# A two-layer trunk on one core: fp32 residual in DRAM, boundary sums on VectorE, a bias table of 32 rows

## The chip, the cores and the metric

The kernel runs on one core of one Trainium2 chip. The metric is the device time of one execution in microseconds (us). The core's engines are TensorE (PE, with its weight loads shown apart as PEld), VectorE (DVE), ScalarE (ACT), GpSimd (POOL) and SyncE (SP); SP, ACT and POOL issue the DMAs.

## The reference

A residual stream h of 512 tokens and 1024 features goes through two layers. The first is a gated linear recurrence (HGRN2), the second differential attention with a relative-position bias; each is followed by a squared-ReLU MLP. Every sub-layer has a norm before and after it. All is float32.

```python
def rms_norm(x, w):
    return x * lax.rsqrt(jnp.mean(x * x, axis=-1, keepdims=True) + EPS) * w

def squared_relu_mlp(h, w_up, w_down):
    u = jax.nn.relu(h @ w_up)
    return (u * u) @ w_down

for layer in range(2):
    if layer == 0:
        mix = hgrn2_mixer(rms_norm(h, a_norm_pre), a_w_in, lb, a_gate_norm, a_w_out)
        h = h + rms_norm(mix, a_norm_post)
    else:
        mix = diff_attn_mixer(rms_norm(h, b_norm_pre), k_sh, v_sh, b_w_q, b_lambda, b_subln, b_w_out, rel_bias, lam_init)
        h = h + rms_norm(mix, b_norm_post)
    ff = squared_relu_mlp(rms_norm(h, mlp_norm_pre[layer]), mlp_w_up[layer], mlp_w_down[layer])
    h = h + rms_norm(ff, mlp_norm_post[layer])
    if layer == 0:
        k_sh, v_sh = shared_kv(h, kv_norm, w_kv)

# in diff_attention, for a block of 128 queries
bias = rel_bias[rel_bucket(k_pos[None, :] - q_pos[:, None])]
logits = q @ k.T * scale + bias          # two maps per head, each with its own softmax
attn = p[:, :, 0] - lam * p[:, :, 1]
```

## The kernel before

Features lie on the partitions and tokens along a row. Every float32 operand of a product is held as two float32r parts, hi and lo, and a product is three matmuls (`mm3`). The residual stream itself is held only as such parts: `xhi[0..3]` and `xlo[0..3]`, each 128 partitions by 2 x 512, so that tile `pr` holds features 256 pr to 256 pr + 255. Weights come from DRAM in pieces of 512 KB on SP's queue into four `raw` buffers (`fetch_w`); ScalarE makes the hi part (`whi`, L172) and VectorE the lo part (`wlo`, L173), into eight buffers each.

The products follow one another in four stages: the mixer of layer 0 with its output products `ao`, the MLP of layer 0 (`up`, then `dn` into `zacc`), the attention with its output products `bo`, the MLP of layer 1. Where a stage ends there is a boundary, done by `bounds`, once for each half of the tokens (h = 0 and 1, 256 tokens each). There are four: ao, m0 (after the first MLP), bo and m1 (after the second MLP, which writes the result; `want` is "out"). Instructions of both m0 and m1 show the name m. A boundary's half goes like this:

- The residual is put together again: `hs = xhi + xlo`, four tiles of 128 x 512, on GpSimd (L268).
- `sums` takes the finished products, squares them on ScalarE and adds the squares (`ssp`): tiles 1 and 2 on GpSimd, tile 3 on VectorE (L290), then the two rows of a tile (L291).
- TensorE turns the squares into a mean on all partitions (`ps_mr`), ScalarE and VectorE make the reciprocal root `ry` (L240 to L252).
- `new` scales the products (L326, two instructions a tile), adds the residual (L327), and splits the sum into xhi (ACT, L331) and xlo (DVE, L332). Of m1's half each, tiles 0 and 1 are added on GpSimd, and the sums go out by DMA (L329).
- `sums` once more, over the new residual (`ssn`), for the next stage's norm: `ps_mr` again, and at m0 also `rb` (ACT, L350) and `ps_rc`.

TensorE's order is written out by `Plan`. It keeps a clock of its own; a chain that waits for other engines yields how long its next product should stay back (the constants W_...), and main work is put in its place. In this order the products of the second token half stand beside the first half's boundary. The other engines' order is made by the scheduler, which prefers instructions of chains (`CHAIN_AHEAD`).

At the start `first_loads` brings x, splits it, and squares it: tiles 0 and 1 on GpSimd (L512), 2 and 3 on ScalarE (L515). The bias of the attention is a row of 640 values for each of 16 maps (`bw`). `params` writes it 128 times over to a DRAM table `bias_dr` of 16 x 128 x 640 by one DMA from GpSimd's queue (L573), while the first MLP runs. `attend` reads it back for each head with a row step of 639, by which each partition gets its row shifted by one more (L834, SP's queue).

Of the kernel before, what the change touches and what calls it, by code (L numbers as in the profile page):

```python
# [17 lines left out]
P = 128  # L18
# [6 lines left out]
NB = 640  # L25
CHAIN_AHEAD = 300

# how long (us) the order of the tensor engine's work leaves a chain to the other engines
W_XSUM, W_XRSTD = 10.0, 6.3                             # x: squares; rstd
W_POST, W_POST_LAST = 4.0, 3.4                          # a post-norm's squares, by half  # L30
W_NEW, W_NEWSUM, W_RSTD = 5.8, 9.7, 4.5                 # new residual: split; squares; rstd
W_GATE_FIRST, W_GATE, W_LEVEL = 10.0, 5.7, 2.15         # recurrence: gates; one level
W_KEYS, W_STATE = 1.5, 0.8                              # recurrence: keys by token; states
W_HEAD, W_STORE = 11.7, 5.5                             # a head's norm; its split
W_QK, W_NEXT, W_P, W_PER_TILE, W_PT = 3.6, 0.94, 5.0, 0.66, 2.5  # attention: q and k; softmax; transposed

# columns of the packed per-feature vectors
# [6 lines left out]
class Plan:  # L44
    """The order of the tensor engine's work: one main stream, and chains that come back to it after a while.

    A generator yields either a number (its next products wait that long, in us, for other engines) or
    a function (it goes on once that is true)."""
# [39 lines left out]
def trunk_kernel(ctx: ExitStack, tc: tile.TileContext, x_t, w_qf, w_g, w_i, w_ao, w_k, w_q, w_v, w_bo, w_up, w_dn,  # L88
# [35 lines left out]
    ulo = [cp.tile([P, 2, S], F32R, name=f"ulo{i}") for i in range(4)]  # L124
    gn = cp.tile([P, G_N], F32, name="gn")
# [20 lines left out]
    bias_dr = dr.tile([16, P, NB], F32, name="bias_dr")  # L146

# [1 line left out]
    def fetch_w(src, ncols, pr, name, pieces=1):  # L149
        """The DMA of 1024 columns' worth of a [128, 8, ncols] block of weights."""  # L150
        per = 1024 // ncols
        raw = wp.tile([P, per, ncols], F32, tag="raw", name=f"raw_{name}_{pr}", bufs=4)
        n = per // pieces
        for i in range(pieces):
            nc.sync.dma_start(raw[:, i * n:(i + 1) * n, :], src[:, per * pr + i * n:per * pr + (i + 1) * n, :])
        return raw

    def split_w(raw, gain, pr, name):
        """Weights (times their gain) in two float32r parts, by rows of 128."""
# [28 lines left out]
    def wmm(ps, wt, kt, c0, xh, xl, lo, hi, start, stop, sk=False):  # L188
        """Weights stationary: ps[feature, token] += w[kt][:, c0:c0+128].T x[kt]."""
        wh, wl = wt[kt]  # L190
        j = kt % 2
        mm3(ps, wh[:, c0:c0 + P], wl[:, c0:c0 + P], xh[kt // 2][:, j, lo:hi], xl[kt // 2][:, j, lo:hi], start, stop, sk)

    def xmm(ps, wt, kt, ncols, t0, start, stop):
        """Tokens stationary: ps[token, feature] += x[kt][:, t0:t0+128].T w[kt]."""
# [4 lines left out]
    def rsqrt_col(ms, add, out, scale=1.0):  # L200
        """out = (ms * scale + add) ** -0.5 on a few columns: a first guess from the exponent, then Newton's steps."""
# [13 lines left out]
    def mean_cols(parts, n, ones):  # L215
        """Sums over the partitions (times ones), tokens on partitions: [128, n / 128] in PSUM."""
# [11 lines left out]
    def mean_rows(parts, n):  # L228
        """Sums over the partitions / D, on every partition: [128, n] in PSUM."""
# [5 lines left out]
    def rsqrt_rows(pool, ms, add):  # L235
        """-2 (ms + add) ** -0.5 on a [128, n] block (add, a block, becomes the sum): a guess from ScalarE's tables, then Newton's step."""
# [18 lines left out]
    def bounds(pool, ps_list, zacc, h, gpost, eab, want, name):  # L255
        """Post-norm of the finished products, residual sum, statistics and split for the next products."""
# [8 lines left out]
        hs = []  # L265
        for pr in range(4):
            r = tl("hs", f"hs{pr}", 4)
            g.tensor_tensor(r, xhs[pr].bitcast(F32), xls[pr].bitcast(F32), op=ALU.add)  # L268
            hs.append(r)

        def sums(src, nm, last=None):
            """Sums of squares over the tiles that src yields (with last: the last tile by halves)."""
            acc = tl("ssum", f"ss{nm}", 2)
            for pr in range(4):
# [14 lines left out]
                if pr > 0:  # L289
                    (v if pr == 3 else g).tensor_tensor(acc, acc, sq, op=ALU.add)  # L290
# [28 lines left out]
        def new(pr, _):  # L319
# [7 lines left out]
            (g if want == "out" and pr < 2 else v).tensor_tensor(t, t, hs[pr], op=ALU.add)  # L327
            if want == "out":
                nc.sync.dma_start(out_t.rearrange("(k p) t -> p k t", p=P)[:, 2 * pr:2 * pr + 2, lo:hi], t)  # L329
                return  # L330
            a.activation(xhs[pr], t, AF.Copy)  # L331
            v.tensor_tensor(xls[pr], t, xhs[pr].bitcast(F32), op=ALU.subtract)  # L332
            return t
# [11 lines left out]
        if want == "ea":  # L345
            # the MLP's products lack the pre-norm's factor: its post-norm takes eps (ms + eps) ** 2 for eps
# [11 lines left out]
    def by_halves(wt, xh, xl, name, before_last=()):  # L358
        """1024 -> 1024 features, weights stationary, tokens by halves: yields between products, keeps the banks."""
        for h, (lo, hi) in enumerate(halves):  # L360
            banks = [mmt(f"{name}_h{h}_{i}") for i in range(4)]
            views = [b.rearrange("p (j t) -> p j t", j=2) for b in banks]
            if h == 1:
                # the last tile in a bank of its own, so that the one before can be read
# [21 lines left out]
    def block(pool, proj, gpost, name, layer, want):  # L386
        """The mixer's output products (proj, from their second half on), its post-norm, and the MLP."""
# [69 lines left out]
    def head_norm(pool, po, add, name):  # L457
        """po [128 tokens, 4, 128 features] in PSUM, normed by token and transposed: [128 features, tokens] in PSUM."""
# [22 lines left out]
    def first_loads(hp):  # L481
        """x and the first head's weights: DMAs, splits and squares, in the order that the products want."""
# [21 lines left out]
        for pr in range(4):  # L504
# [5 lines left out]
            if pr < 2:  # L510
                sq.append(hp.tile([P, 2, S], F32, tag="vt", name=f"sqx{pr}", bufs=2))
                g.tensor_tensor(sq[pr], raws[pr], raws[pr], op=ALU.mult)  # L512
            else:
                sq.append(raws[pr])
                a.activation(sq[pr], raws[pr], AF.Square)  # L515
# [4 lines left out]
    def start(hp, ssum, maskf):  # L520
        """The statistics of x, and the lower bound of the gates."""
        # lower bound of the forget gate: running sum of a softmax over the layers, less its first row
# [12 lines left out]
        # as a row of tokens on every partition  # L535
# [8 lines left out]
    def params(hp):  # L544
        # small parameters of the attention layer
# [27 lines left out]
        nc.gpsimd.dma_start(bias_dr, bw.unsqueeze(1).to_broadcast([16, P, NB]))  # L573
        done("par")

    def hgrn(hp, w0):
        apre = gn[:, G_APRE:G_APRE + 8]

        def gate(ps, tag, name):
            """z = ps * rb, and sigmoid(z)."""  # L580
# [6 lines left out]
        def head(h, pss):  # L587
# [6 lines left out]
            # by chunk: its queries, and its odd ones one step on  # L594
# [9 lines left out]
            # scores [key, query] inside each chunk; then the keys of the first three chunks, by token  # L604
# [3 lines left out]
            def between(li, s, to, ps):  # L608
                """The scores of the even blocks' keys with the odd blocks' queries, from PSUM."""
# [49 lines left out]
            # the state after each chunk, and what each chunk takes from the one before it  # L659
# [74 lines left out]
    def attention_first(f):  # L734
        """Keys, queries and values of the first two heads, by token halves, left in PSUM."""
# [15 lines left out]
    def attention(ap, f):  # L751
        top, low = slice(0, 64), slice(64, P)

        def slots(h):
            """Room for a head's keys and queries in float32r parts: five tiles of [128, 512]."""
# [6 lines left out]
        def keep_k(ks, ps):  # L762
            """Normed keys, a tile for each map: high parts in the map's own rows, low parts in the other's."""
# [220 lines left out]
```

## Time and profile before

| | |
|---|---|
| runs (us) | 1345.91, 1347.38, 1350.63; median 1347.38 |
| profiled execution, its span | 1347.3 us |
| DMA traffic | 120.11 MB, mean 89 GB/s |
| on GpSimd's queue | 5.24 MB in 1040 packets |
| instructions on GpSimd | 135, busy 123.5 us |
| granted clock of TensorE | 0.98 of full speed in the mean |

The profile is that of one execution. Its page has the busy time of each engine, the groups of instructions by line, the DMA issues, and the chain of work that ended last. Answers of the trace add the waits of one engine with what released it, the timeline of one engine in a window, and the busy time and granted clock in windows. In a timeline row stand the start, the duration, the engine, the line, the operation, the tile written and the tiles read, and in brackets the idle time ahead of it with what ended it. Tile names lose their buffer numbers there.

### The profile page before, as it was taken

Reading aid. Unit: us, or ns where it says so; the run is one execution under the profiler, and the core shown is the slowest. Engines: PE = TensorE matmul, PEld = TensorE weight load, DVE = VectorE, ACT = ScalarE, POOL = GpSimd, SP = SyncE. Lnnn points to the kernel's source line nnn. Section 1 sums busy time; section 2 is a strip of 40 time slices with the busy share of each in tenths; the row PEclk is TensorE's granted clock in tenths of the full one; section 3 lists DMA queues with packets and bytes.
Section 4 is the critical chain, followed back from the end, with each engine's and each line's share of the span. In section 5 each row is a group of like instructions: output and inputs, shape, how many; then the busy total and the mean of one; then the engine's idle time right before and its main releaser. Section 6 shows DMA issues by size and latency. Waiting matters only on the chain.

```text
span 1347.3 us, 19315 instructions
## 1 busy us (share of the span) xinstructions
PE 1290.8 (96%) x7586; PEld 1121.9 (83%) x7586; DVE 798.1 (59%) x1674; ACT 574.4 (43%) x1189; POOL 123.5 (9%) x135
## 2 busy tenths in 40 slices
PE   8999999998999799999998999999889999999996
PEld 6889898998887678888988888889888888888895
DVE  7987777659643253525288988673975343444336
ACT  6553534336332232414245887663643241432322
POOL 1110101024100000000040000001320000000004
PEclk9999999998999899999998999999889999999998
DMA  6322212103136941313104422220304222232201
GB/s 224 114 79 63 79 64 79 63 4 126 63 125 74 171 161 63 125 63 125 63 3 140 140 99 66 88 94 1 126 19 153 79 95 93 95 110 83 87 1 63
DMA packets 36060, 120.11 MB, mean 89 GB/s; under 512 B 3809, under 2 KB 6114, under 8 KB 35970
## 3 DMA queue, kind: packets, MB, share of 16 engines
q1 hardware_dynamic: 34688, 113.52, 25.0%
q0 software_dynamic: 1040, 5.24, 3.5%
q8 instruction: 59, 0.97, 0.3%
q14 instruction: 31, 0.25, 0.1%
q10 hardware_dynamic: 242, 0.13, 0.0%
HBM read 111.54 MB, written 7.34 MB: 88 GB/s over the span
## 4 chain that ended last, share of the span: by engine, by line
PE 80%; DVE 10%; DMA 6%; ACT 2%; issue 2%; SPq 0%; DVEq 0%; ACTq 0%
PE up L113 21%; PE dn L113 20%; PE kq L113 6%; PE qf L113 6%; PE dn_h L113 5%; PE g L113 4%; DMA raw_dn<-in_w_dn_dram 4%; PE v L113 3%; PE i L113 3%; PE gl L113 3%; PE ao_h L113 2%; PE bo_h L113 2%; DVE xlo L332 2%; PE lg L113 2%; PE ao L113 1%
## 5 line engine op out<-in xcount | busy, mean ns | idle before, releaser
L113 PE MATMUL up<-xhi,whi_up 128*128 128x512 f32 (+1 forms) x640 | 227.9, 356 | 7.2 <-ACT r L400 7.2
L113 PE MATMUL up<-xlo,whi_up 128*128 128x512 f32 (+1 forms) x640 | 226.5, 354 | 0.0
L113 PE MATMUL up<-xhi,wlo_up 128*128 128x512 f32 (+1 forms) x640 | 226.0, 353 | 0.0
L172 ACT ACTIVATE whi_up<-raw_up,gn 128x512 fp32r<-128x512 f32 x128 | 86.1, 716 | 198.8 <-issue 124.3
L113 PE MATMUL dn<-uhi,whi_dn 128*128 128x512 f32 x384 | 152.1, 396 | 1.8 <-ACT r L400 1.8
L113 PE MATMUL dn<-ulo,whi_dn 128*128 128x512 f32 x384 | 151.9, 395 | 0.0
L113 PE MATMUL dn<-uhi,wlo_dn 128*128 128x512 f32 x384 | 151.9, 395 | 0.0
L113 PEld LDWEIGHTS up<-xhi,whi_up 128*128 128x128 f32 x640 | 123.2, 193 | 25.4 <-ACT r L400 7.7
L113 PEld LDWEIGHTS up<-xlo,whi_up 128*128 128x128 f32 x640 | 123.1, 192 | 17.8
L113 PEld LDWEIGHTS up<-xhi,wlo_up 128*128 128x128 f32 x640 | 123.0, 192 | 17.6
L173 DVE SCALAR_TENSOR_TENSOR wlo_up<-raw_up,gn,whi_up 128x512 fp32r<-128x512 f32 x128 | 94.1, 779 | 71.6 <-ACT whi_up L172 71.6
L401 DVE TENSOR_TENSOR r<-r 128x512 f32<-128x512 f32 x64 | 44.1, 689 | 126.3 <-ACT r L400 126.3
L165 DVE TENSOR_TENSOR wlo_dn<-raw_dn,whi_dn 128x1024 fp32r<-128x1024 f32 x64 | 76.5, 1222 | 40.6 <-ACT whi_dn L164 39.5
L400 ACT ACTIVATE r<-up 128x512 f32<-128x512 f32 x64 | 37.8, 590 | 133.8 <-PE up L113 133.8
L113 PEld LDWEIGHTS dn<-uhi,whi_dn 128*128 128x128 f32 x384 | 72.2, 188 | 19.7 <-ACT r L400 2.2
L113 PEld LDWEIGHTS dn<-uhi,wlo_dn 128*128 128x128 f32 x384 | 72.2, 188 | 17.4
L113 PEld LDWEIGHTS dn<-ulo,whi_dn 128*128 128x128 f32 x384 | 72.2, 188 | 17.3
L164 ACT ACTIVATE whi_dn<-raw_dn 128x1024 fp32r<-128x1024 f32 x64 | 66.6, 1055 | 40.6 <-DMA raw_dn<-in_w_dn_dram 23.6
L113 PE MATMUL dn_h<-uhi,whi_dn 128*128 128x256 f32 x240 | 67.8, 282 | 0.0
L113 PE MATMUL dn_h<-uhi,wlo_dn 128*128 128x256 f32 x240 | 67.4, 281 | 0.0
L113 PE MATMUL dn_h<-ulo,whi_dn 128*128 128x256 f32 x240 | 67.4, 281 | 0.0
L403 DVE TENSOR_TENSOR ulo<-r,uhi 128x512 fp32r<-128x512 f32 x64 | 46.4, 724 | 30.7 <-ACT uhi L402 30.7
(329 smaller groups left out, 2994.6 us busy)
## 6 DMA issues: line engine op xcount, KB each, us to landing
raw_up<-in_w_up_dram SPq DMA_DIRECT2D x64, 512.0 KB, 3.5
raw_dn<-in_w_dn_dram SPq DMA_DIRECT2D x64, 512.0 KB, 4.7
raw_qf<-in_w_qf_dram SPq DMA_DIRECT2D x15, 512.0 KB, 3.7
bias_dr<-bw POOLq DMA_DIRECT2D x1, 5120.0 KB, 57.0
raw_wi<-in_w_i_dram SPq DMA_DIRECT2D x8, 512.0 KB, 3.5
raw_wg<-in_w_g_dram SPq DMA_DIRECT2D x8, 512.0 KB, 3.6
raw_ao<-in_w_ao_dram SPq DMA_DIRECT2D x8, 512.0 KB, 3.5
raw_wk<-in_w_k_dram SPq DMA_DIRECT2D x8, 512.0 KB, 3.5
```

The costliest lines, as they stand in the source:

```text
L113: nc.tensor.matmul(out, lhsT, rhs, **kw)
L164: a.activation(hi, raw, AF.Copy)
L165: v.tensor_tensor(lo, raw, hi.bitcast(F32), op=ALU.subtract)
L172: a.activation(hi[:, j, :], raw[:, j, :], AF.Copy, scale=gc)
L173: v.scalar_tensor_tensor(lo[:, j, :], raw[:, j, :], gc, hi[:, j, :].bitcast(F32), op0=ALU.mult, op1=ALU.subtract)
L332: v.tensor_tensor(xls[pr], t, xhs[pr].bitcast(F32), op=ALU.subtract)
L400: a.activation(r, psv, AF.Relu)
L401: v.tensor_tensor(r, r, r, op=ALU.mult)
L403: v.tensor_tensor(uv_l, r, uv_h.bitcast(F32), op=ALU.subtract)
```

## The change

The residual is kept in DRAM in float32. A list `res` holds for each token half where it lies: at first the input, then a DRAM tile `res_ao`, `res_m` or `res_bo`. In place of the sum on GpSimd, `bounds` loads four tiles `rs` of 256 KB (as large as `hs`, and as many), by DMAs from GpSimd's queue. VectorE adds the scaled products into `rs`, and the sum goes from there to xhi and xlo and, by another DMA from GpSimd's queue, to DRAM; the last boundary stores nothing back and sends `rs` out. All additions of squares, and all of the last boundary's sums, are on VectorE. The squares of x are all on ScalarE. The bias table has 32 rows a map instead of 128, and a head's tile is read by four DMAs of 32 partitions each. Beside this the diff removes comments.

```diff
+NREP = 32
...
+    res = [x_t.rearrange("(k p) t -> p k t", p=P)[:, :, lo:hi] for lo, hi in ((0, 256), (256, 512))]
...
-    bias_dr = dr.tile([16, P, NB], F32, name="bias_dr")
+    bias_dr = dr.tile([16, NREP, NB], F32, name="bias_dr")
...
-        hs = []
+        rs = []
         for pr in range(4):
-            r = tl("hs", f"hs{pr}", 4)
-            g.tensor_tensor(r, xhs[pr].bitcast(F32), xls[pr].bitcast(F32), op=ALU.add)
-            hs.append(r)
+            rs.append(tl("rs", f"rs{pr}", 4))
+            g.dma_start(rs[pr], res[h][:, 2 * pr:2 * pr + 2, :])
+        if want != "out":
+            res[h] = dr.tile([P, 8, n], F32, name=f"res_{name}{h}")
...
                 if pr > 0:
-                    (v if pr == 3 else g).tensor_tensor(acc, acc, sq, op=ALU.add)
+                    v.tensor_tensor(acc, acc, sq, op=ALU.add)
...
-            (g if want == "out" and pr < 2 else v).tensor_tensor(t, t, hs[pr], op=ALU.add)
+            r = rs[pr]
+            v.tensor_tensor(r, t, r, op=ALU.add)
             if want == "out":
-                nc.sync.dma_start(out_t.rearrange("(k p) t -> p k t", p=P)[:, 2 * pr:2 * pr + 2, lo:hi], t)
+                nc.sync.dma_start(out_t.rearrange("(k p) t -> p k t", p=P)[:, 2 * pr:2 * pr + 2, lo:hi], r)
                 return
-            a.activation(xhs[pr], t, AF.Copy)
-            v.tensor_tensor(xls[pr], t, xhs[pr].bitcast(F32), op=ALU.subtract)
-            return t
+            a.activation(xhs[pr], r, AF.Copy)
+            v.tensor_tensor(xls[pr], r, xhs[pr].bitcast(F32), op=ALU.subtract)
+            g.dma_start(res[h][:, 2 * pr:2 * pr + 2, :], r)
+            return r
...
-            if pr < 2:
-                sq.append(hp.tile([P, 2, S], F32, tag="vt", name=f"sqx{pr}", bufs=2))
-                g.tensor_tensor(sq[pr], raws[pr], raws[pr], op=ALU.mult)
-            else:
-                sq.append(raws[pr])
-                a.activation(sq[pr], raws[pr], AF.Square)
+            sq.append(hp.tile([P, 2, S], F32, tag="vt", name=f"sqx{pr}", bufs=2) if pr < 2 else raws[pr])
+            a.activation(sq[pr], raws[pr], AF.Square)
...
-        nc.gpsimd.dma_start(bias_dr, bw.unsqueeze(1).to_broadcast([16, P, NB]))
+        nc.gpsimd.dma_start(bias_dr, bw.unsqueeze(1).to_broadcast([16, NREP, NB]))
...
-            src = bass.AP(bias_dr.tensor, bias_dr.offset + 2 * h * P * NB + 127, [[NB - 1, P], [P * NB, 2], [1, S]])
-            nc.sync.dma_start(bt, src)
+            for r in range(0, P, NREP):
+
+                src = bass.AP(bias_dr.tensor, bias_dr.offset + 2 * h * NREP * NB + 127 - r,
+                              [[NB - 1, NREP], [NREP * NB, 2], [1, S]])
+                nc.sync.dma_start(bt[r:r + NREP], src)
```

TensorE's order is the same in both kernels. GpSimd's queue is not. At the boundary ao it held these rows before, from the first half's residual sums on (numbers behind a name are those of the buffers; two tiles of one name with different numbers are different tiles or halves):

```order
L268 TENSOR_TENSOR hs_ao_2970<-xhi_66,xlo_70 128x512
L268 TENSOR_TENSOR hs_ao_2972<-xhi_67,xlo_71 128x512
L268 TENSOR_TENSOR hs_ao_2974<-xhi_68,xlo_72 128x512
L268 TENSOR_TENSOR hs_ao_2976<-xhi_69,xlo_73 128x512
L290 TENSOR_TENSOR ssp_ao_2982<-ssp_ao_2982,sqp_ao_2985 128x512
L290 TENSOR_TENSOR ssp_ao_2982<-ssp_ao_2982,sqp_ao_2989 128x512
L268 TENSOR_TENSOR hs_ao_3303<-xhi_66,xlo_70 128x512
L268 TENSOR_TENSOR hs_ao_3305<-xhi_67,xlo_71 128x512
L290 TENSOR_TENSOR ssn_ao_3046<-ssn_ao_3046,sqn_ao_3053 128x512
L268 TENSOR_TENSOR hs_ao_3307<-xhi_68,xlo_72 128x512
L290 TENSOR_TENSOR ssn_ao_3046<-ssn_ao_3046,sqn_ao_3061 128x512
L268 TENSOR_TENSOR hs_ao_3309<-xhi_69,xlo_73 128x512
```

In the changed kernel the same place holds only DMA issues (rs are the tiles loaded, res_ao the DRAM tile of a half; 2970 to 2976 are the first half's tiles, 3308 to 3314 the second's):

```order
L271 DMA rs_ao_2970<-in_x_t_dram 128x2x256
L271 DMA rs_ao_2972<-in_x_t_dram 128x2x256
L271 DMA rs_ao_2974<-in_x_t_dram 128x2x256
L271 DMA rs_ao_2976<-in_x_t_dram 128x2x256
L338 DMA res_ao_2978<-rs_ao_2970 128x512
L338 DMA res_ao_2978<-rs_ao_2972 128x512
L271 DMA rs_ao_3308<-in_x_t_dram 128x2x256
L338 DMA res_ao_2978<-rs_ao_2974 128x512
L271 DMA rs_ao_3310<-in_x_t_dram 128x2x256
L271 DMA rs_ao_3312<-in_x_t_dram 128x2x256
L338 DMA res_ao_2978<-rs_ao_2976 128x512
L271 DMA rs_ao_3314<-in_x_t_dram 128x2x256
```

The sums became loads, the additions of squares left the queue, and a load of the second half stands behind the store that frees its buffer.

VectorE's queue at the same boundary, first half, from the last tiles' scaling to the end of the new residual's squares, before (raw, whi and wlo are a weight piece and its parts):

```order
L326 SCALAR_TENSOR_TENSOR z_ao_2981<-z_ao_2981,gnh,ry 128x256
L173 SCALAR_TENSOR_TENSOR wlo_up_0_0_3238<-raw_up_0_0_3235,gn,whi_up_0_0_3237 128x512
L332 TENSOR_TENSOR xlo_72<-z_ao_2980,xhi_68 128x2x256
L327 TENSOR_TENSOR z_ao_2981<-z_ao_2981,hs_ao_2976 128x512
L173 SCALAR_TENSOR_TENSOR wlo_up_0_0_3238<-raw_up_0_0_3235,gn,whi_up_0_0_3237 128x512
L173 SCALAR_TENSOR_TENSOR wlo_up_0_1_3246<-raw_up_0_1_3243,gn,whi_up_0_1_3245 128x512
L332 TENSOR_TENSOR xlo_73<-z_ao_2981,xhi_69 128x2x256
L290 TENSOR_TENSOR ssn_ao_3046<-ssn_ao_3046,sqn_ao_3069 128x512
L291 TENSOR_TENSOR ssn_ao_3046<-ssn_ao_3046 128x256
L173 SCALAR_TENSOR_TENSOR wlo_up_0_1_3246<-raw_up_0_1_3243,gn,whi_up_0_1_3245 128x512
```

and of the changed kernel:

```order
L294 TENSOR_TENSOR ssn_ao_3047<-ssn_ao_3047,sqn_ao_3055 128x512
L337 TENSOR_TENSOR xlo_72<-rs_ao_2974,xhi_68 128x2x256
L294 TENSOR_TENSOR ssn_ao_3047<-ssn_ao_3047,sqn_ao_3064 128x512
L330 SCALAR_TENSOR_TENSOR z_ao_2982<-z_ao_2982,gnh,ry 128x256
L176 SCALAR_TENSOR_TENSOR wlo_up_0_0_3243<-raw_up_0_0_3240,gn,whi_up_0_0_3242 128x512
L332 TENSOR_TENSOR rs_ao_2976<-z_ao_2982,rs_ao_2976 128x512
L176 SCALAR_TENSOR_TENSOR wlo_up_0_0_3243<-raw_up_0_0_3240,gn,whi_up_0_0_3242 128x512
L176 SCALAR_TENSOR_TENSOR wlo_up_0_1_3251<-raw_up_0_1_3248,gn,whi_up_0_1_3250 128x512
L337 TENSOR_TENSOR xlo_73<-rs_ao_2976,xhi_69 128x2x256
L294 TENSOR_TENSOR ssn_ao_3047<-ssn_ao_3047,sqn_ao_3073 128x512
L294 TENSOR_TENSOR ssp_ao_3321<-ssp_ao_3321,sqp_ao_3324 128x512
L295 TENSOR_TENSOR ssn_ao_3047<-ssn_ao_3047 128x256
```

Two additions of squares (L294) came in ahead of the last tile, the first one of the second half's products stands ahead of the final sum (L295), and the addition of the residual writes the tile rs.

## The prediction

> **What bounds the kernel now.** I read the page first, then the waits of TensorE, then the stretches of half clock, then the chain and the timeline of the engines that TensorE waits for.
>
> ```profile
> span 1347.3 us, 19315 instructions
> PE 1290.8 (96%) x7586; PEld 1121.9 (83%) x7586; DVE 798.1 (59%) x1674; ACT 574.4 (43%) x1189; POOL 123.5 (9%) x135
> ```
>
> TensorE (PE) is busy 96% of the span, and the order of its instructions is the same before and after. So the change can only touch the time in which PE stands idle and the time in which it runs at a lower clock. The profiled execution spans 1347.3 us, the median of the three runs is 1347.38: nothing lies around the span, and I sum against 1347.3.
>
> The view of PE's waits gives, for each product and what released it, the total in us, the number of waits and the longest:
>
> ```profile
> PE ps_mr L113 <- DVE ssn_bo L291: 10.8, 2, 5.9
> PE ps_mr L113 <- DVE ssn_ao L291: 8.2, 2, 4.8
> PE up L113 <- ACT r L400: 7.2, 1, 7.2
> PE qf L113 <- DVE xlo L507: 4.1, 3, 1.9
> PE ps_rc L113 <- ACT rb L350: 3.9, 1, 3.9
> PE ps_mr L113 <- DVE ssn_m L291: 3.3, 1, 3.3
> PE dn L113 <- ACT r L400: 1.8, 1, 1.8
> ...
> PE bo_h L113 <- ACT uhi L478: 0.7, 1, 0.7
> ```
>
> Three places hold nearly all of it: the boundaries ao, m0 and bo (10.8 + 8.2 + 3.9 + 3.3), where PE waits for the sums of squares of the new residual; one spot in the first MLP (7.2 + 1.8); and the start (4.1). The longer of these waits cost a second time. The rows below are windows of the trace just behind them: the stretch, PE busy, the other engines, and the granted clock.
>
> ```profile
> 316.53:323.36 6.83, 5.55 (x24) 5.37 (x25) 6.83 (x11) 4.70 (x10) 0.94 (x1) 0.50 0.54 164
> 347.25:350.66 3.41, 3.41 (x14) 3.23 (x15) 1.22 (x2) 1.10 (x2) 0.00 (x0) 0.50 0.02 5
> 463.30:470.13 6.83, 3.58 (x8) 2.82 (x9) 3.12 (x4) 2.88 (x5) 0.00 (x0) 0.50 0.99 166
> 712.48:719.30 6.82, 5.71 (x22) 5.34 (x23) 5.45 (x16) 5.62 (x15) 0.00 (x0) 0.50 0.55 190
> 958.24:965.06 6.82, 3.96 (x16) 3.79 (x17) 6.79 (x10) 4.79 (x10) 1.78 (x2) 0.50 0.36 102
> ```
>
> PE was busy 5.55 + 3.41 + 3.58 + 5.71 + 3.96 = 22.2 us at a granted clock of 0.50. At full clock that work takes about half, so some 11 us more hang on the waits. The wait of 3.3 at ssn_m left no such stretch, those of 3.4 and more did.
>
> **Why PE waits at a boundary.** Rows of the timeline of VectorE (DVE) and GpSimd (POOL) at ao (start, duration):
>
> ```profile
> 302.56 0.68 DVE L327 TENSOR_TENSOR z_ao<-z_ao,hs_ao 128x512 f32<-128x512 f32 x1
> ...
> 305.00 1.78 DVE L327 TENSOR_TENSOR z_ao<-z_ao,hs_ao 128x512 f32<-128x512 f32 x1
> ```
> ```profile
> 300.29 1.47 POOL L268 TENSOR_TENSOR hs_ao<-xhi,xlo 128x512 f32<-128x512 f32 x1 [6.33 <-DVE z_ao L327]
> ...
> 304.75 1.48 POOL L290 TENSOR_TENSOR ssn_ao<-ssn_ao,sqn_ao 128x512 f32<-128x512 f32 x1
> ...
> 315.94 1.53 POOL L290 TENSOR_TENSOR ssp_ao<-ssp_ao,sqp_ao 128x512 f32<-128x512 f32 x1 [0.74 <-ACT sqp_ao L285]
> ```
> ```profile
> 331.86 1.47 POOL L268 TENSOR_TENSOR hs_m<-xhi,xlo 128x512 f32<-128x512 f32 x1 [14.39 <-DVE z_ao L327]
> ...
> 343.44 1.65 POOL L268 TENSOR_TENSOR hs_m<-xhi,xlo 128x512 f32<-128x512 f32 x1 [1.24 <-DVE z_ao L327]
> ```
>
> The same addition takes 0.68 us alone and 1.78 us when a POOL addition runs beside it, and it then ends when that one does. From 300.29 to 315.94 there are 8 POOL additions and 8 stretched DVE instructions, in the second half (331.86 to 343.44) 6 and 6. Taking 1.04 us for one, a little under the 1.10 of this pair, POOL adds 8.3 us to DVE's chain in the first half and 6.2 in the second. That the other boundaries are alike is seen in the groups by line (mean in ns; alone the same form takes about 680):
>
> ```profile
> L332 DVE TENSOR_TENSOR xlo<-z_ao,xhi 128x512 fp32r<-128x512 f32 x8 | 9.6, 1199 | 0.1
> L332 DVE TENSOR_TENSOR xlo<-z_bo,xhi 128x512 fp32r<-128x512 f32 x8 | 9.6, 1198 | 0.1
> ...
> L332 DVE TENSOR_TENSOR xlo<-zacc,xhi 128x512 fp32r<-128x512 f32 x8 | 8.7, 1091 | 0.0
> ```
>
> **The change, part by part.** It takes 66 computing instructions from POOL: 32 sums hs, 28 additions of squares, 4 additions of the output, 2 squares of x. It puts 56 DMA issues there, 32 residual loads and 24 stores. DVE gets 32 additions at a pitch of 0.60 us (0.68 with the overlap of the next).
>
> *ao, first half.* DVE loses 8 stalls, 8.3 us, and gains ahead of the wait's end two additions for ssn and one for ssp, 1.8 us: the chain ends 6.5 us sooner, the wait was 4.8. Gone, with 1.7 to spare. With it goes half of the 5.55 us at half clock, 2.8.
>
> *ao, second half.* PE now comes 4.8 + 2.8 = 7.6 us sooner. The chain's head hangs on a weight load that follows the first half's DVE work; that ends 8.3 less five additions (3.0) = 5.3 sooner, and its own six stalls less two additions give 5.0. The wait of 3.4 becomes 3.4 + 7.6 - 10.3 = 0.7, and 1.7 of half clock goes.
>
> *bo.* The same in the first half: 4.8 and 2.0 (half of 3.96) go. In the second the wait was 5.9; PE comes 6.8 sooner, the chain 10.3: 2.4 stay. It is more than at ao because the weight load in this chain took 6.66 instead of 4.75 (rows below). The wait at bo_h, 0.7, goes too: there POOL's first sums run beside the last head's norm on DVE.
>
> *m0.* The wait of 3.3 goes: I count 7 stalls, one fewer than at ao (its lower mean of 1091 bears that out), 7.3; less three additions they leave 5.5. The 3.9 for rb hangs on a load of raw_wv behind the same DVE work; PE comes 3.3 sooner, the chain 5.5 plus one later stall less its addition: 3.9 + 3.3 - 5.9 = 1.3 stay at most, I take 1.0. Half of 5.71 goes, 2.9.
>
> *Bias table.* Pieces of the chain, and the DMA issues (size, us to landing):
>
> ```profile
> 311.12 0.60 DVE z_ao L327
> ...
> 321.10 4.75 DMA raw_up<-in_w_up_dram
> ...
> 331.18 0.60 DVE z_ao L327
> ...
> 423.12 34.06 DMA raw_dn<-in_w_dn_dram
> ...
> 459.63 14.35 DMA raw_dn<-in_w_dn_dram
> ...
> 964.38 6.66 DMA raw_up<-in_w_up_dram
> ```
> ```profile
> bias_dr<-bw POOLq DMA_DIRECT2D x1, 5120.0 KB, 57.0
> ...
> out_dram<-zacc SPq DMA_DIRECT2D x8, 256.0 KB, 2.2
> ```
>
> ```profile
> 414.62 1.18 POOL L573 DMA_DIRECT2D bias_dr<-bw  x1 [69.53 <-PE dn L113]
> ```
>
> Beside the 57 us in which the table is written, weight loads hold the chain for 34.06 and 14.35 us instead of 4 to 7, and the second ends at 474.0, where the write ends too (414.6 + 1.2 + 57.0 = 472.8). A quarter of the bytes at the same rate takes 14 us: the write ends 43 us sooner, and PE lacked weights for 9.0. I take the whole: 7.2 + 1.8 + half of 3.58 = 10.8. The four loads per head instead of one cost SP three issues each; no wait in the attention is over 0.7, so nothing falls due there; I take 1.0 for all heads, between 0 and 24 loads at 2.2 = 53 if none were hidden, nearest to the loads that are hidden now.
>
> *Tail and start.*
>
> ```profile
> 1337.88 4.63 DVE zacc L322 x4
> 1342.51 0.60 DVE zacc L327
> ```
> ```profile
> 7.81 1.90 DVE L507 TENSOR_TENSOR xlo<-raw_x,xhi 128x512 fp32r<-128x512 f32 x1 [1.43 <-ACT xhi L506]
> ```
> ```profile
> 17.15 1.06 ACT L515 ACTIVATE raw_x<-raw_x 128x1024 f32<-128x1024 f32 x1 [3.54 <-DVE xlo L507]
> ```
>
> In the tail four products take 4.63 instead of 4 x 0.60, for two POOL additions, and two DVE additions follow: 5.8 us. After, four products and four additions take 4.8: 1.0 less. At the start xlo no longer takes 1.90 beside POOL's squares (0.68 is usual for its size), but ScalarE gets two squares of 1.06 ahead of later xhi: between 0 and the whole 4.1; I take 1.5, since 2.1 us of squares eat about half.
>
> *The new waits.* A residual tile must land before its addition. The first half's loads have nothing ahead of them but a free buffer. Those of the second half go into buffers that the stores must leave first: an issue, a landing, an issue, a landing, by the rows 2 x 1.18 + 2 x 2.2 = 6.8 us, against 20 us between the first half's last addition (311.12) and the second half's first (331.18), which both move by about five. Queued behind a waiting POOL issue are only further residual transfers, and the memsets of bt much later. I price it at 0; the other end is rival D. For traffic beside the weight loads I take 1.0, between 0 and 2.0 per boundary (6.66 against 4.75).
>
> **Sum.** Removed: bias 10.8; ao 8.2 + 4.5 = 12.7; m0 7.2 + 2.9 = 10.1; bo 10.8 + 2.0 + 0.7 = 13.5; start 1.5; tail 1.0: 49.6. Left over or new: 0.7 + 2.4 + 1.0 + 1.0 + 1.0 = 6.1. Gain 43.5: 1347.3 - 43.5 = **1303.8**.
>
> **Rivals.** *B: the boundaries stay bound by DVE and the weights.* DVE has little room there, its additions grow by 0.60 each, and residual traffic makes loads like the 6.66 the rule. If half of the boundary terms (36.3) stays, the time is 1303.8 + 18.2 = 1322. For it speaks that waits of 0.7 to 2.4 remain in my own sum; against it the spare 1.7 and 2.2 us in the first halves.
>
> *C: a DMA issue on POOL holds DVE as an addition did.* This ends slower. The issue of the bias took 1.18. Each of the three boundaries would have about 16 issues, 18.9 us of stalls, and six more additions on DVE, 3.6 us, instead of 14 x 1.04 = 14.6: 7.9 longer, 24 for three. Against it stand bias, start, tail and bo_h, 14.0: 1347.3 + 24 - 14.0 = 1357. It decides from about 0.98 us per issue (48 x 0.98 = 14.0 + 3 x 14.6 - 3 x 3.6). Against it speaks a POOL memset that ran inside a DVE instruction with two inputs, which took its usual time:
>
> ```profile
> 743.91 0.20 POOL L835 MEMSET bt<- 64x128 f32 x1 [13.43 <-DMA bt<-bias_dr]
> ```
> ```profile
> 743.73 0.69 DVE L776 TENSOR_TENSOR kq<-qf,ulo 64x512 fp32r<-64x512 f32 x1
> ```
>
> So not every POOL instruction stalls DVE; that an issue does not is a choice of mine. [...]
>
> *D: the residual lands late.* No row shows a POOL DMA issued under a busy DVE. It decides from a landing of (20 - 2.4) / 2 = 8.8 us. With the 14.35 that raw_dn took beside the table's write, the pair of store and load takes 31 us, and the second halves of ao, m0 and bo lose 11 each: 1303.8 + 33 = 1337. Against it: 2.2 us is what a transfer of this size takes. [...]
>
> *E: the bias part does nothing,* if the weights are late there for another reason: 10.8 stay, 1315. The 34.06 beside the 57.0 speaks against it.
>
> **Chances.** Forecast 0.64 (own range 1295 to 1310: nothing left over and the start's other 2.6, or twice what is left over), B 0.18, D 0.06, C 0.06, E 0.06. The range 1295 to 1325 takes in the forecast's own, E and most of B, and leaves out C, D and the upper end of B, some 0.2. A measurement tells 0.3%, 4 us, from no change. Faster 0.92, same 0.02, slower 0.06.
>
> **What would show it.** Right: no PE wait over 3 us at ps_mr; DVE's xlo at about 0.68 throughout; raw_dn landing within 15 us near 420; no half clock after the start. Wrong: DVE instructions of 1.2 us or more beside POOL issues (C), additions L332 that wait for a DMA of rs (D), the chain through raw_up at the boundaries (B).

## The result and the profile after

The changed kernel takes 1310.99 us (median of four runs, 1309.72 to 1312.45), the kernel before 1346.74 (median of four runs, the three of the table above and one more): the ratio is 0.9725, 95% interval 0.9707 to 0.9742. The forecast was 1303.8 in a range of 1295 to 1325. The way and the range were right; some 6 us of the expected gain are missing, and the time lies 1 us outside the forecast's own range of 1295 to 1310. The profiled execution spans 1309.7 us against 1347.3.

From the page of the changed kernel (engine, busy time, instructions), and from the view of TensorE's waits:

```profile
span 1309.7 us, 19433 instructions
PE 1282.2 (98%) x7586; PEld 1115.7 (85%) x7586; DVE 762.7 (58%) x1706; ACT 574.9 (44%) x1191; POOL 57.7 (4%) x125
```
```profile
PE v L114 <- DVE wlo_wv L176: 4.9, 2, 3.4
PE ps_mr L114 <- DVE ssn_bo L295: 2.8, 1, 2.8
PE ps_mr L114 <- DVE ssn_ao L295: 2.2, 1, 2.2
...
PE bo_h L114 <- ACT uhi L484: 0.7, 1, 0.7
```

The waits of the first halves, of the bias table and of `rb` are gone. Two second halves wait on, and there is a wait that the kernel before did not have: the first value products `v` stand still for 4.9 us. A window just behind it (PE busy, and at its end clock, DMA share and GB/s) shows half clock, too:

```profile
697.00:704.00 7.00, 5.64 (x28) 5.64 (x29) 6.01 (x14) 1.15 (x2) 0.54 (x1) 0.53 0.58 195
```

A second stretch at half clock, from 956.1 to 959.5, follows the wait at the second half of bo.

Since TensorE's order did not change, the gain can be told stage by stage. A stage runs from the first product of one name to the first of the next, in the two traces (us); the forecast's terms are put where they belong:

| stage | before | after | forecast | measured |
|---|---|---|---|---|
| start, recurrence, to ao_h | 262.3 | 259.5 | -1.5 | -2.8 |
| ao, to the first dn | 111.2 | 100.9 | -12.0 | -10.3 |
| first MLP with the bias table, to dn_h | 281.6 | 270.5 | -10.8 | -11.1 |
| m0, to the first lg | 91.7 | 89.4 | -9.1 | -2.3 |
| attention, to bo_h | 151.9 | 151.9 | +1.0 | 0.0 |
| bo, to the next dn | 119.9 | 109.5 | -11.1 | -10.4 |
| second MLP | 268.8 | 268.8 | 0 | 0.0 |
| m1 and the end | 59.9 | 59.2 | -1.0 | -0.7 |

With the 1.0 for traffic beside the weight loads, which is spread over ao and bo, the forecast's column gives -43.5, the measured one -37.6. All but one stage come within 2 us; m0 lacks 6.8.

What VectorE does now, in its groups by line (mean in ns in the last column but one), and a store's issue on GpSimd beside two products on VectorE (start, duration):

```profile
L337 DVE TENSOR_TENSOR xlo<-rs_ao,xhi 128x512 fp32r<-128x512 f32 x8 | 5.5, 686 | 0.1
L337 DVE TENSOR_TENSOR xlo<-rs_bo,xhi 128x512 fp32r<-128x512 f32 x8 | 5.5, 684 | 0.1
L337 DVE TENSOR_TENSOR xlo<-rs_m,xhi 128x512 fp32r<-128x512 f32 x8 | 5.5, 682 | 0.2 <-ACT xhi L336 0.2
```
```profile
297.76 0.57 POOL L338 DMA_DIRECT2D res_ao<-rs_ao  x1 [27.65 <-DVE rs_ao L332]
```
```profile
297.38 0.88 DVE L330 SCALAR_TENSOR_TENSOR z_ao<-z_ao,gnh,ry 128x256 f32<-128x256 f32 x2
```

The same two products in the kernel before, beside an addition on GpSimd:

```profile
303.17 1.92 DVE L326 SCALAR_TENSOR_TENSOR z_ao<-z_ao,gnh,ry 128x256 f32<-128x256 f32 x2
```

The subtraction that took 1091 to 1199 ns in the mean now takes 682 to 686, as alone (0.68 at 301.96 in the kernel before, with GpSimd idle). Two products in a row take 0.88 with an issue beside them instead of 1.92 beside an addition. In the kernel before, 25 of VectorE's instructions over tiles of 128 x 512 took more than 1.0 us; in the changed kernel none takes more than 0.9, and 21 of its 24 subtractions run beside an issue. These issues, of 0.54 to 0.88 us, did not hold VectorE. The transfers (KB, us to landing):

```profile
rs_ao<-in_x_t_dram POOLq DMA_DIRECT2D x8, 256.0 KB, 3.9
res_ao<-rs_ao POOLq DMA_DIRECT2D x8, 256.0 KB, 3.0
...
bias_dr<-bw POOLq DMA_DIRECT2D x1, 1280.0 KB, 14.9
```

### The profile page after: what moved, and what is told of

Its sections match the earlier page's. It is cut to its first block, busy times and chain, and to the rows that moved or that the text cites. A ratio compares the mean times of both kernels' runs of the same rounds, so it can differ in the third digit from the quotient of the medians.

```text
span 1309.7 us, 19433 instructions
## 1 busy us (share of the span) xinstructions
PE 1282.2 (98%) x7586; PEld 1115.7 (85%) x7586; DVE 762.7 (58%) x1706; ACT 574.9 (44%) x1191; POOL 57.7 (4%) x125
## 4 chain that ended last, share of the span: by engine, by line
PE 86%; DVE 6%; ACT 4%; DMA 2%; issue 1%; SPq 0%; DVEq 0%; ACTq 0%
PE up L114 24%; PE dn L114 21%; PE kq L114 6%; PE qf L114 6%; PE dn_h L114 5%; PE g L114 4%; PE v L114 3%; PE i L114 3%; PE gl L114 3%; PE bo_h L114 2%; PE ao_h L114 2%; PE lg L114 2%; PE ao L114 1%; DMA raw_up<-in_w_up_dram 1%; PE o L114 1%
## 5 line engine op out<-in xcount | busy, mean ns | idle before, releaser
L114 PE MATMUL up<-xhi,whi_up 128*128 128x512 f32 (+1 forms) x640 | 225.2, 352 | 0.0
L114 PE MATMUL dn<-ulo,whi_dn 128*128 128x512 f32 x384 | 151.9, 395 | 0.0
L114 PE MATMUL dn<-uhi,wlo_dn 128*128 128x512 f32 x384 | 151.9, 395 | 0.0
L176 DVE SCALAR_TENSOR_TENSOR wlo_up<-raw_up,gn,whi_up 128x512 fp32r<-128x512 f32 x128 | 90.4, 747 | 76.0 <-ACT whi_up L175 76.0
```

What stands on the lines that cost most here:

```text
L114: nc.tensor.matmul(out, lhsT, rhs, **kw)
L176: v.scalar_tensor_tensor(lo[:, j, :], raw[:, j, :], gc, hi[:, j, :].bitcast(F32), op0=ALU.mult, op1=ALU.subtract)
```

## The experiments

Twelve kernels were run beside the kernel before. Each interval belongs to the ratio to it.

**One part of the change alone, or left out.** First the bias table alone (`NREP = 32` and the four loads per head in the kernel before), and the changed kernel without it:

```diff
-NREP = 32
+NREP = 128
```

> The kernel before with the table of 32 rows and four loads per head alone; the residual sums and the sums of squares stay on GpSimd. Theory (the parts add up, the bias term is 10.8 us): about 1336 us, the wait of 7.2 before an up product and the half clock near 463 gone, the waits at the boundaries (8.2 at ao, 10.8 at bo, 3.3 + 3.9 at m0) as before. Rival (the weights near 420 are late for another reason): 1347, the wait of 7.2 stays.

> The changed kernel with the table of 128 rows again and one load per head. Theory (parts add up): 1311 + 11 = 1322 us, with the wait of about 7 and its half clock back near 450. Rival (the earlier PE needs the weights at another time, so the long write falls beside something else): within 4 us of 1311.

The table alone: 1336.87 us, ratio 0.9912 (0.9881 to 0.9942). All but the table: 1323.53, ratio 0.9808 (0.9778 to 0.9839). The stage with the table takes 270.5 us in the first and 281.8 in the second, against 281.6 before and 270.5 after; no other stage moves by over 1.6 us against its base. The parts add up, and the table's term is 11.1 where 10.8 was forecast. With the table alone the waits at the boundaries stay, though not all at their old size (8.2 us at bo instead of 10.8, and 1.7 instead of 3.9 for `rb`, which was not expected); without it the old wait in the first MLP is back:

```profile
PE ps_mr L114 <- DVE ssn_ao L292: 8.4, 2, 4.8
PE ps_mr L114 <- DVE ssn_bo L292: 8.2, 2, 4.8
```
```profile
PE up L114 <- ACT r L406: 7.4, 1, 7.4
```

**The new wait at v.** In the changed kernel's timeline of VectorE at m0, the last pieces of the first value weights stand among the second half's work (rows left out between are of both kinds):

```profile
688.12 0.47 DVE L176 SCALAR_TENSOR_TENSOR wlo_wv<-raw_wv,gn,whi_wv 128x256 fp32r<-128x256 f32 x1
688.51 1.27 DVE L330 SCALAR_TENSOR_TENSOR zacc<-zacc,gnh,ry 128x256 f32<-128x256 f32 x3
...
695.62 0.48 DVE L176 SCALAR_TENSOR_TENSOR wlo_wv<-raw_wv,gn,whi_wv 128x256 fp32r<-128x256 f32 x1
...
697.83 0.47 DVE L176 SCALAR_TENSOR_TENSOR wlo_wv<-raw_wv,gn,whi_wv 128x256 fp32r<-128x256 f32 x1
```

TensorE stopped at 692.8 and went on behind the last two of these rows, at 696.2 and 698.4. The raw weights had landed at 685.44 (a chain piece of 5.34 us from 680.09), and ScalarE had their hi parts ready at 687.5. In the kernel before all eight pieces stood ahead of the second half. Two causes were open, VectorE's order and the late load:

```diff
-        f["wv"] = load_w(w_v[0], 256, gn[:, G_KV:G_KV + 8], "wv0")
+        with tc.high_priority(offset=CHAIN_AHEAD):
+            f["wv"] = load_w(w_v[0], 256, gn[:, G_KV:G_KV + 8], "wv0")
```

> The changed kernel, but the split of the first value weights (wv0) has the priority of a chain, so that VectorE has all eight wlo_wv pieces behind it before it starts on the second half of boundary m0; in the changed kernel the last two stand inside that half. TensorE's, GpSimd's and SyncE's orders are those of the changed kernel. Theory (the new waits before the v products, 3.36 + 1.58 us and the half clock behind them, 7.8 us together, come from VectorE's order alone): the waits go, 1311 - 7.8 = 1303 us, perhaps 1 more where the second half ends later. Rival (raw_wv lands late, 5.34 us, beside the residual's traffic): the wait stays within 1 us, 1310 to 1311.

It took 1306.32 us, ratio 0.9685 (0.9659 to 0.9712). The profiled run, with a span of 1302.4, is the fastest of six. The waits at v are gone; m0 takes 83.5 us instead of 89.4, 8.1 less than before the change (forecast: 9.1). The eight pieces now end ahead of the second half:

```profile
684.01 1.69 DVE L176 SCALAR_TENSOR_TENSOR wlo_wv<-raw_wv,gn,whi_wv 128x256 fp32r<-128x256 f32 x4 [0.41 <-ACT whi_wv L175]
```

The orders of TensorE, GpSimd and SyncE are those of the changed kernel, and the slowest landing of raw_wv did not get shorter (5.9 us, 5.3 before this edit): VectorE's order was the cause. The gain is 5.8 of the 7.8 us expected at this place. The next products `kq` now wait 0.7 and 0.3, which is half of the difference; the rest stays open. Another 1.0 us of the shorter span lies at bo, where a wait of 3.3 us was not followed by half clock in this execution.

**What stalls VectorE.** To the changed kernel 24 GpSimd instructions are added that nobody needs, behind each residual addition at ao, m0 and bo; `t` is a tile that is dead by then. Once they read nothing, once they read two operands:

```diff
+            g.memset(t, 0.0)
             g.dma_start(res[h][:, 2 * pr:2 * pr + 2, :], r)
```
```diff
+            g.tensor_tensor(t, r, r, op=ALU.add)
             g.dma_start(res[h][:, 2 * pr:2 * pr + 2, :], r)
```

> The changed kernel with 24 GpSimd memsets of 128 x 512 added, one behind each residual addition at ao, m0 and bo, into the scaled tile that nobody reads any more. They read nothing. Theory (a GpSimd instruction stalls VectorE only where it reads on-chip memory, whatever its length): 1311 us within 3, VectorE's additions beside a memset stay at 0.68. Rival (any GpSimd instruction of this length stalls VectorE): like the additions, 1325 to 1335.

> As the run with memsets, but each of the 24 is a GpSimd addition of two tiles (r + r) into the same dead tile, whose result nobody reads. Theory (the stalls alone made the boundaries late): 24 stalls of about 1.04 us come back, 8 a boundary; after the first halves' slack of 1.7 and with half clock, some 5 us a boundary, 1321 to 1333 us. Rival (the boundaries were late because VectorE waited for GpSimd's results): nobody waits for these, so 1311 within 3.

With the memsets 1312.51 us, ratio 0.9742 (0.9727 to 0.9756), span 1309.5: no change. With the additions 1329.01, ratio 0.9867 (0.985 to 0.9883), span 1326.9: 17.2 us more than the changed kernel, 0.7 for each addition. VectorE is busy for 780.1 us with the additions and 762.2 with the memsets: 17.9 more, 0.75 for each. The same two products beside a memset (first two rows) and beside an addition (last two):

```profile
299.65 0.53 POOL L338 MEMSET z_ao<- 128x512 f32 x1 [0.85 <-DVE rs_ao L332]
```
```profile
299.45 0.87 DVE L330 SCALAR_TENSOR_TENSOR z_ao<-z_ao,gnh,ry 128x256 f32<-128x256 f32 x2
```
```profile
301.15 1.14 POOL L338 TENSOR_TENSOR z_ao<-rs_ao 128x512 f32<-128x512 f32 x1 [1.12 <-DVE rs_ao L332]
```
```profile
300.91 1.65 DVE L330 SCALAR_TENSOR_TENSOR z_ao<-z_ao,gnh,ry 128x256 f32<-128x256 f32 x2
```

No engine waits for the result of either, no VectorE addition waits for a residual load, and but for these 24 instructions the orders of all engines are the same in both runs. The boundaries were late because of the stalls. In the kernel before VectorE did also wait for GpSimd's `ssp` (4.5 us at ao, 6.5 at bo), but the chain that ended last holds no work of GpSimd's. The memsets are shorter (0.53 against 1.14), so a part of the difference could be length; but at 0.53 their stalls would still show, and 0.87 has none: three such products take 1.28 in the changed kernel with GpSimd idle (at 943.19). So GpSimd's additions, which read two operands, held VectorE for 0.75 us each, and its memsets, of 0.53 us here and 0.20 in the kernel before, did not. That the reading alone decides, whatever the length, was the author's theory; no run has a memset as long as an addition.

**Where the residual sum is made.** The residual again as xhi + xlo, nothing of it in DRAM, once on VectorE and once on GpSimd; the sums of squares stay on VectorE:

```diff
-            g.dma_start(rs[pr], res[h][:, 2 * pr:2 * pr + 2, :])
+            v.tensor_tensor(rs[pr], xhs[pr].bitcast(F32), xls[pr].bitcast(F32), op=ALU.add)
...
-            g.dma_start(res[h][:, 2 * pr:2 * pr + 2, :], r)
```
```diff
+            g.tensor_tensor(rs[pr], xhs[pr].bitcast(F32), xls[pr].bitcast(F32), op=ALU.add)
```

> The changed kernel without the residual in DRAM: hs = xhi + xlo again, as 32 additions on VectorE, no residual loads or stores. Theory (what counts is that GpSimd does no additions; DRAM only spares VectorE 4 x 0.60 us a half): the second halves of ao and bo end up to 2.4 to 4.8 us later, 1314 to 1321 us. Rival (the residual's DMA traffic, which stretches the weight loads at ao and bo to 6.3 and 6.9 us, costs as much as the additions): 1311 or less, with those loads back at 4.5 to 5 us.

> The changed kernel without the residual in DRAM: hs = xhi + xlo on GpSimd as before, the sums of squares and the output's sums on VectorE as in the change. Theory: 8 stalls of 1.04 a boundary remain, and VectorE keeps the added additions: ao and bo lose about 8 us each against the changed kernel, m0 about 4, 1325 to 1335 us; the last boundary's too. Rival (moving the sums of squares was what mattered): 1311 to 1316.

On VectorE 1317.28 us, ratio 0.9763 (0.9732 to 0.9794); the span is 3.4 us longer than the changed kernel's (6.3 by the medians), 1.6 of it at m0 and 1.2 at ao. DRAM is worth a few us; most of the boundary gain comes without it. On GpSimd 1332.05, ratio 0.9886 (0.9871 to 0.99): ao and bo lose 9.0 and 7.2 us against the changed kernel, m0 3.7; the last boundary, which was expected to lose too, did not (58.9 us, 59.2 in the changed kernel). All orders but GpSimd's are those of the changed kernel here, so what costs this are 32 additions on GpSimd in place of its 56 transfers. Its waits:

```profile
PE ps_mr L114 <- DVE ssn_bo L293: 7.3, 2, 5.9
PE ps_mr L114 <- DVE ssn_ao L293: 6.9, 2, 5.4
```

**The squares of x.** In the changed kernel tiles 0 and 1 are squared on GpSimd again:

```diff
-            a.activation(sq[pr], raws[pr], AF.Square)
+            if pr < 2:
+                g.tensor_tensor(sq[pr], raws[pr], raws[pr], op=ALU.mult)
+            else:
+                a.activation(sq[pr], raws[pr], AF.Square)
```

> The changed kernel with the squares of x's first two tiles on GpSimd again. Theory (those two squares stall VectorE's xlo and wlo at the start): the start is 2.8 us longer as in the kernel before, 1313 to 1314 us, xlo of 1.9 us and waits of 1.4 and 1.9 before qf back. Rival (the start gained by other means): 1311.

1314.63 us, ratio 0.9755 (0.9742 to 0.9769); the first stage takes 262.3 us, as before the change. xlo of this run, and of the changed kernel:

```profile
7.98 1.90 DVE L513 TENSOR_TENSOR xlo<-raw_x,xhi 128x512 fp32r<-128x512 f32 x1 [1.56 <-ACT xhi L512]
```
```profile
8.05 0.69 DVE L513 TENSOR_TENSOR xlo<-raw_x,xhi 128x512 fp32r<-128x512 f32 x1 [1.07 <-ACT xhi L512]
```

**The queue of the residual's transfers.** All 56 on SyncE's queue, among the weight loads:

```diff
-            g.dma_start(rs[pr], res[h][:, 2 * pr:2 * pr + 2, :])
+            nc.sync.dma_start(rs[pr], res[h][:, 2 * pr:2 * pr + 2, :])
...
-            g.dma_start(res[h][:, 2 * pr:2 * pr + 2, :], r)
+            nc.sync.dma_start(res[h][:, 2 * pr:2 * pr + 2, :], r)
```

> The changed kernel with all 56 residual DMAs on SyncE's queue instead of GpSimd's, among the weight loads. Theory (the loads and stores on GpSimd's queue land in 2.6 to 4.0 us and nobody waits for them; on SyncE a store that waits for its addition holds the weight loads behind it): same or slower, 1311 to 1330 us. [...]

The theory lost: 1305.71 us, ratio 0.9692 (0.9678 to 0.9707), span 1303.6. But the landings changed little: in the medians loads land after 3.2 to 3.7 us and stores after 2.1 to 3.2, from GpSimd after 3.4 to 4.0 and 2.6 to 3.4. The gain lies at bo (3.6) and ao (1.2). In the changed kernel GpSimd's queue at bo reads:

```profile
925.40 0.54 POOL L271 DMA_DIRECT2D rs_bo<-res_m  x1 [3.06 <-DVE wlo_up L176]
925.93 0.54 POOL L338 DMA_DIRECT2D res_bo<-rs_bo  x1
931.03 0.54 POOL L271 DMA_DIRECT2D rs_bo<-res_m  x1 [4.56 <-ACT ea L353]
```

and the last sum of this half on VectorE, and the last weight load in the chain:

```profile
923.39 0.68 DVE L332 TENSOR_TENSOR rs_bo<-z_bo,rs_bo 128x512 f32<-128x512 f32 x1
```
```profile
932.20 6.93 DMA raw_up<-in_w_up_dram
```

The load in the first row stood 3 us in the queue; its buffer's store had landed at 924.8. The last store stood behind it, 1.9 us after its sum was done (924.07), and the last load, which needs that store's buffer, went out at 931.03, just ahead of the weight load, which took 6.93. Not all of that need be the residual's: with no residual transfers at all this load took 6.66 in the kernel before and 5.52 with the residual summed on VectorE.

A new theory: it is the order within GpSimd's queue, not that GpSimd issues. Then moving either the stores or the loads away should be enough. Three runs with the value weights first, which differ from that version on GpSimd's and SyncE's queues alone:

> The value weights' split first and all residual DMAs on SyncE's queue: the two versions that were faster than the changed kernel, together. VectorE's, ScalarE's and TensorE's orders are those of the version with the value weights first. Theory (the two gains lie in different places, 8 us less at m0 and 4 to 5 at the second halves of ao and bo): about 1301 us, the waits at v gone and those at ao and bo at 1.0 and 0.6. Rival (they share a cause, a late weight load): 1304 to 1306.

> The value weights first, the residual's 24 stores on SyncE, its 32 loads still on GpSimd. Theory (order in GpSimd's queue: a store whose sum is ready stands there behind a load that waits for a buffer, so the last load comes 5 us late and falls beside the last raw_up piece, which lands after 6 to 7 us): with the stores out of that queue the loads go sooner, raw_up lands in about 5 us, the second halves wait 1 us or less, 1301 to 1303. Rival (a transfer issued by GpSimd lands late as such): loads are still there, no more than half of the gain, 1304 to 1306.

> The value weights first, the residual's 32 loads on SyncE, its 24 stores on GpSimd. Theory (order in the queue): the stores no longer stand behind loads, the loads stand among the weight loads: 1301 to 1304, waits at the second halves of ao and bo under 2 us. Rival (a transfer issued by GpSimd lands late as such): half of the gain, 1304 to 1306.

| moved to SyncE | us | ratio, interval | span | ao | bo |
|---|---|---|---|---|---|
| nothing (value weights first) | 1306.32 | 0.9685, 0.9659 to 0.9712 | 1302.4 | 100.3 | 108.5 |
| loads and stores | 1300.79 | 0.9651, 0.9638 to 0.9664 | 1298.7 | 98.8 | 106.5 |
| the stores | 1302.19 | 0.9659, 0.9646 to 0.9673 | 1298.0 | 98.8 | 105.9 |
| the loads | 1300.67 | 0.9651, 0.9638 to 0.9664 | 1298.8 | 98.9 | 105.9 |

Spans and stages are those of one profiled execution each. Each of the two moves alone brings all of it, within the scatter of the runs. With the stores moved, the last load still comes from GpSimd, but 4.0 us ahead of the last weight load instead of 1.2, and the weights then take 4.79 (a row of the queue, a piece of the chain):

```profile
920.32 0.54 POOL L271 DMA_DIRECT2D rs_bo<-res_m  x1 [4.80 <-DMA res_bo<-rs_bo]
```
```profile
924.34 4.79 DMA raw_up<-in_w_up_dram
```

By the ratios these versions are 0.7 to 0.8% faster than the changed kernel.

## Why the prediction was right, and where it was not

**What bounds the kernel: right.** TensorE's order stood, and its idle time fell with the waits. Of six stretches at half clock between start and tail (the five counted and one at the second half of bo) one is left, the sixth, and one at v is new. The price of half of such a stretch agrees with two windows of the kernel before: 14 products in 3.40 us at 0.50 (992.37 to 995.80), 27 in 3.38 at 1.00 (703.7 to 707.1). **The stall by GpSimd's additions: right, and shown** by the runs with memsets and additions. Its price of 1.04 us was for additions of 1.3 to 1.6 us (means of their groups); the 24 added ones, of 1.17 to 1.21, cost VectorE 0.75 each, and the end time nearly all of it, 0.7. The prediction has the stretched instruction end when the addition beside it does; in the pair shown GpSimd's ends at 306.23 and VectorE's at 306.78, 0.55 later.

**ao and bo: right in kind,** 10.3 and 10.4 us for 12.0 and 11.1. Both first halves lost their waits whole. The second halves waited 2.2 and 2.8 us where 0.7 and 2.4 were left. The step that was mis-sized is the one on the new waits, which priced the residual's traffic at 1.0 in all and saw nothing wrong in GpSimd's queue, where "only further residual transfers" wait behind a waiting issue. These were enough: a store held up by a load put the next load beside the weight load. The half clock at the second half of bo was not in the sum. The window that was read there, 988.96 to 992.37, holds only the idle half of the stretch; TensorE worked at half clock in the other half, and does so at the same place in the changed kernel:

```profile
992.37:995.80 3.43, 3.40 (x14) 3.22 (x15) 1.28 (x2) 1.10 (x2) 0.00 (x0) 0.50 0.00 0
```
```profile
956.10:959.50 3.40, 3.40 (x19) 3.40 (x18) 0.92 (x2) 1.52 (x3) 0.54 (x1) 0.50 0.24 58
```

The sum missed about 1.7 us that the kernel before lost here and the same that the changed kernel still loses. The two cancel, which is luck.

**The wait at bo_h: wrong.** It was credited to GpSimd's first sums, and it is 0.7 in every run. The stalls there went and VectorE is earlier, so they were not what TensorE waited for. A likely reason is that TensorE's written order puts these products directly behind the last head's transposes, with ScalarE's split between them; no run tests it.

**m0: this is the step that failed.** The wait for `rb` went as forecast, and "1.3 stay at most, I take 1.0" looked for the next late thing in that same chain. The next late thing was other work: the scheduler had put two pieces of wlo_wv inside VectorE's second half, where all stood ahead of it before, and the v products that need them wait 4.9 us and then run at half clock. With VectorE's order put right m0 gains 8.1 us for 9.1 forecast, and the version's span of 1302.4 is 1.4 below the forecast time. That closeness is in part luck: it is the fastest run of six, their median of 1306.32 lies 2.5 above, and what ao and m0 lack is made good by the start, by the loads per head that cost nothing, and by the half clock that did not come at bo.

**The bias table, tail and start.** 11.1 for 10.8; 0.7 for 1.0; 2.8 for 1.5, since TensorE's waits for xlo and xhi at the start fell from 4.4 to 1.5 although ScalarE got the two squares. The extra loads per head cost nothing where 1.0 was set. The end of the table's write was put at 472.8; the 57.0 count from the start of the issue, so it is 471.6, which changes no term.

**The rivals.** C (issues hold VectorE) is refuted by the rows above, and its price was too high besides: an issue of the residual takes 0.54 to 0.88 us, not the 1.18 of the one large transfer. D (late landings) did not come in its form: no addition waited for a residual load, and the longest landing of one was 6.6 us, under the 8.8 from which D decides. E is refuted by the run with the table alone. B was in part what happened: weight loads at the second halves of ao and bo.

**The signs.** Three of the four signs of being right came: no wait over 2.8 us at ps_mr, xlo at 0.68, and raw_dn landing within 12.8 us. The fourth, no half clock after the start, did not.

## What to carry to other kernels

Before a VectorE chain is blamed for being long, look for instructions of one form with two lengths (0.68 and 1.78 us here), and for what GpSimd does at that time; additions of 1.17 to 1.21 us that GpSimd did for nothing cost VectorE here 0.75 each, about two thirds of their length. When a wait is removed, walk the order of each engine a few products past it: here two pieces of wlo_wv came next, and cost a wait of 4.9 us. And look for what stands behind a transfer that waits: in GpSimd's queue here a load that stood for 3 us had a store behind it whose sum was done, 1.9 us before the store went out, and with the stores or the loads on SyncE's queue the time fell from 1306.32 to 1302.19 or 1300.67. So loads that wait and stores that don't are worth trying on two queues.

## What the runs showed of the hardware

- 24 GpSimd memsets of 0.53 us beside VectorE's chain changed the span by 0.2 us; 24 additions of 1.17 to 1.21 us (means of their groups) changed it by 17.2.
- A small VectorE instruction with one tile as input was held too: a row of 128 x 4 took 1.22 us beside one of GpSimd's sums in the kernel before, and 0.20 in the changed kernel:

```profile
923.39 1.22 DVE L209 TENSOR_SCALAR yh<-nx 128x4 int32<-128x4 int32 x1
```
```profile
896.78 0.20 DVE L212 TENSOR_SCALAR yh<-nx 128x4 int32<-128x4 int32 x1
```

- Residual transfers of 256 KB landed nearly as fast from GpSimd's queue (medians of 2.6 to 4.0 us) as from SyncE's (2.1 to 3.7). VectorE was busy beside them: 13.51 of 13.51 us from 916.91 to 930.42 in the changed kernel, while seven of them went out from GpSimd and landed after 2.3 to 4.5 us.
- The length of an idle stretch did not decide by itself whether half clock followed. One of 2.75 us (ps_mr at the second half of bo in the changed kernel) was followed by 0.50 from 956.1 to 959.5; one of 3.3 at the same place, with the value weights first, by full clock (1.00 from 949.6 to 953.0). One of 3.31 us (ps_mr at m0 in the kernel before) was followed by full clock; one of 3.3 us at the same place, with the bias table changed alone, by a stretch at 0.50 from 693.5 to 697.0:

```profile
693.50:697.00 3.50, 3.48 (x14) 3.30 (x15) 3.50 (x7) 2.85 (x8) 1.39 (x1) 0.50 0.16 16
```
